# z and h as pairs of blocks, the first chunk's sums a tile later, and h turned between the units of the last chunk, in a hybrid encoder block of split fp32 matmuls

## The chip, the core and the metric

The kernel runs on one core of one Trainium2 chip. TensorE does the matmuls, and it also turns (transposes) blocks by multiplying them with the identity. VectorE and ScalarE make operands for it and empty its PSUM banks, GpSimd takes a few helper jobs, and SyncE issues most of the DMAs. Each engine works through its own instructions in the order in which they stand. The metric is the device time of one execution in microseconds (us), lower is better. Times shown are medians of runs, the profiled execution is one run more.

## The reference, cut to what matters

```python
D_MODEL, SEQ, D_FF = 2048, 512, 4 * 2048

def rms_norm(x, gain):
    return x * lax.rsqrt(jnp.mean(x * x, axis=-1, keepdims=True) + EPS) * gain

def reference(...):
    h = x
    ...                       # gated convolutions: mixed
    o = jnp.einsum("bse,ed->bsd", mixed, w_out)
    h = h + rms_norm(o, mix_post_gain)
    m = rms_norm(h, mlp_pre_gain)
    z = jnp.square(jax.nn.relu(jnp.einsum("bsd,df->bsf", m, w_up)))
    z = jnp.einsum("bsf,fd->bsd", z, w_down)
    return h + rms_norm(z, mlp_post_gain)
```

All is float32. Tokens are 512, so that a block of 128 features by 512 tokens takes 256 KB, 2 KB on each of 128 partitions.

## The kernel before, in words

**Numbers.** Every float32 operand is split into a high part (ScalarE rounds it, L94 for activations, L237 for weights) and a low part (VectorE subtracts, L95 and L242). A product is three matmuls: high by low, low by high, high by high.

**Stages.** Input projection, convolutions, output projection, up projection, down projection. The up projection gives z in 64 blocks of 128 features by 512 tokens. Most of them are made two at a time by Strassen's scheme with seven products (`by_seven`, products in L296). After the last sum ScalarE takes relu and square and stores each block to `z_dram` on its own queue (`relu_squared`). The 16 blocks of h had gone to `h_dram` in the same layout, features on partitions.

**Down projection.** It has features of the output on the free axis: the stationary operand is a block of z (128 features by 128 tokens), the moving one 512 columns of w_down. Its 64 z blocks go in 8 chunks of 8.

- Chunks 0 to 6: two tiles of the output (`wide_tile`, t = 0 and 1: 4 banks for the 4 groups of 128 tokens, 8 blocks, so 8 x 4 x 3 = 96 matmuls in L889 to L891), then the other half of the output by seven products (`wide_seven`, 7 x 24 matmuls). A unit of weights is 128 x 1024, two blocks; each unit of a `wide_tile` is 24 matmuls. After a tile the banks are copied (chunk 0) or added (later) to the running totals.
- The seven products also need sums of neighbouring blocks of z, `t_z`, four pairs in a chunk. `strassen_sums` (L332) makes them on VectorE from a pair of blocks that `load_pair` (L883) loads from DRAM once more, and splits them (L94, L95). `chunk_block` orders this: while tile t = 0 takes its blocks, it loads a pair at one block and makes its sums at the next.
- The blocks of z for a chunk are loaded one by one into `scratch` (256 KB, 8 buffers named tmp) by `load_z` (L824) and split two steps later. `prepare_z` lists these steps for the next chunk, and `z_step(n)` does n of them: three after each of the seven products, for chunk 0 within the last seven products of the up projection.
- The last chunk takes four `wide_tile`s with its first four blocks (8 units of 24 matmuls) and then, after h has been turned, the final part: for each group of 128 tokens b and each tile t, four blocks (12 matmuls), the last sum, and for each b the norm and the writing of the output.
- h is wanted with tokens on partitions. So between the last chunk's tiles and the final part come four transposes of the norm (L1000) and 64 of h: 16 loads of one block (L1017, into tmp), per bank four transposes (L1021), then one ScalarE copy into a slot (L1025).

**What sets the order.** No scheduler moves anything: each engine executes its instructions in the order in which the program writes them, and `evacuate` puts an evacuation off to the next `run_pending`. SyncE issues all loads of weights, z and h on one queue in that order; a load waits there until its buffer is free, and all behind it wait too. Weights go through 6 buffers named raw (L122). `W.take(n, AHEAD)` hands out n units and prepares units up to AHEAD further on. PSUM has 7 banks, and there are 43 slots of 4 KB per partition for split operands, sums and totals. The few rows named `small` and the identity are from pools of their own or from scratch.

Of the kernel before, what the change touches and what calls it, by code (L numbers as in the profile page):

```python
# [13 lines left out]
P = 128  # L14
# [44 lines left out]
def encoder_block(  # L59
# [279 lines left out]
    def evacuate(f, *args):  # L339
        pending.append(lambda: f(*args))  # L340
# [478 lines left out]

    z, z_raw = {}, {}  # L820

    def load_z(k):
        z_raw[k] = scratch()
        nc.sync.dma_start(z_raw[k], z_dram[:, k * S : (k + 1) * S])  # L824

    def split_z(k):
        z[k] = split_pair(z_raw.pop(k))
# [2 lines left out]

    def prepare_z(c):

        for i in range(CHUNK + 2):
            for f, behind in ((load_z, 0), (split_z, 2)):
                if 0 <= i - behind < CHUNK:
                    z_steps.append(lambda f=f, k=c * CHUNK + i - behind: f(k))

    def z_step(n):
        while n > 0 and z_steps:
            z_steps.popleft()()  # L840
            n -= 1
# [9 lines left out]
    for m in range(UP_PLAIN, N_UP, 2):  # L851
        if m == N_UP - 2:
            prepare_z(0)
            evacuate(z_step, 2)
        by_seven(
            up_product,
            *(scratch() for _ in range(2)),
            *((lambda c, m=n: relu_squared(m, c, c)) for n in (m, m + 1)),
            z_step,
        )  # L860
# [15 lines left out]
            for i in range(2):  # L876
                total[t, 2 * n + i] = pair[:, i, :]

    def load_pair(c, i):
        pair = scratch(), scratch()  # L880
        for n, t in enumerate(pair):
            k = c * CHUNK + 2 * i + n
            nc.sync.dma_start(t, z_dram[:, k * S : (k + 1) * S])  # L883
        return pair

    def wide(ps, z_hi, z_lo, part, n, first, last):

        hi, lo = (w[:, n * WIDE : (n + 1) * WIDE] for w in part)
# [3 lines left out]

    tokens = lambda n: slice(n * P, (n + 1) * P)

    def wide_tile(t, first_sum, blocks, make_moving, step):

        pss = [bank() for _ in range(TB)]
        for n in range(0, len(blocks), 2):
            (part,) = W.take(1, AHEAD)
            run_pending()  # L900
            for i in range(2):
                moving = make_moving(blocks[n + i])
                for b, ps in enumerate(pss):
                    wide(
                        ps, *both(moving, tokens(b)), part, i,
                        n + i == 0, n + i == len(blocks) - 1,
                    )
            step()
        for b, ps in enumerate(pss):
            evacuate(accumulate, first_sum, total[t, b], ps)  # L910

    def wide_seven(c):

        if c == 0:
            for _ in range(7):
                seven.append(slot([P, 2, WIDE]))
        for q, name in enumerate(("r10", "t10", "t11", "t20", "t21", "r21", "r20")):
            parts = W.take(2, AHEAD)
            run_pending()
            n, half = int(name[1]) - 1, int(name[2]) * TB // 2  # L920
            right = lambda i: z[c * CHUNK + 2 * i + n] if name[0] == "r" else t_z[i][n]
            for j in range(2):
                ps = bank()
                for i in range(CHUNK // 2):
                    wide(
                        ps, *both(right(i), tokens(half + j)), parts[i // 2], i % 2,
                        i == 0, i == CHUNK // 2 - 1,
                    )
                evacuate(accumulate, c == 0, seven[q][:, j, :], ps)
            z_step(3)  # L930

    def combine():
        p1, p5, p6, p7, p4, p3, p2 = seven
# [8 lines left out]
            total[3, j], total[3, 2 + j] = p4[:, j, :], p7[:, j, :]  # L942
        return deque(steps)

    AHEAD = 4
    run_pending()
    for c in range(N_CHUNK):
        pairs = deque(range(CHUNK // 2))
        waiting = []

        def chunk_block(k):
            while c * CHUNK + k not in z:
                z_step(1)
            if c < N_CHUNK - 1:
                if waiting:
                    i, even, odd = waiting.pop()
                    t_z[i] = strassen_sums(even, odd)
                elif pairs:
                    i = pairs.popleft()
                    waiting.append((i, *load_pair(c, i)))  # L960
            return z[c * CHUNK + k]

        if c == N_CHUNK - 1:
            break
        for t in range(2):
            if c == 0:
                new_total(t)
            wide_tile(t, c == 0, range(CHUNK), chunk_block, lambda: None)
        prepare_z(c + 1)
        wide_seven(c)  # L970


    steps = combine()

    def combine_step():
        for _ in range(4):
            if steps:
                pending.append(steps.popleft())

    for t in range(N_WIDE):  # L980
        wide_tile(t, False, range(CHUNK // 2), chunk_block, combine_step)

    gains = [slot([P, 2, WIDE]) for _ in range(2)]
    for n, t in enumerate(gains):
# [3 lines left out]
            .partition_broadcast(P)  # L988
            .rearrange("p o (a b) -> p (o a) b", a=2),
        )  # L990
    identity = scratch(P)
    nc.gpsimd.memset(identity, 1.0)
    nc.gpsimd.affine_select(
        out=identity, in_=identity, pattern=[[1, P]], compare_op=ALU.is_equal, fill=0.0, base=0,
        channel_multiplier=-1,
    )
    norm_2, norm_4 = (new(small, [P, TB], F32, "four") for _ in range(2))
    ps = bank()
    for b in range(TB):
        nc.tensor.transpose(ps[:, tokens(b)], norm["h 2"][:, tokens(b)], identity)  # L1000
    for b in range(TB):
        nc.scalar.activation(norm_2[:, b : b + 1], ps[:, b * P : b * P + 1], AF.Copy)
    nc.vector.tensor_tensor(norm_4, norm_2, norm_2, op=ALU.mult)
# [6 lines left out]
    h_back = {}  # L1010

    def turn(t):

        h = [scratch() for _ in range(4)]
        for i in range(4):
            k = 4 * t + i
            nc.sync.dma_start(h[i], h_dram[:, k * S : (k + 1) * S])  # L1017
        for b in range(TB):
            ps = bank()
            for i in range(4):  # L1020
                nc.tensor.transpose(ps[:, tokens(i)], h[i][:, tokens(b)], identity)  # L1021
            if b % 2 == 0:
                pair = slot([P, 2, WIDE])
            h_back[t, b] = pair[:, b % 2, :]
            nc.scalar.activation(h_back[t, b], ps, AF.Copy)  # L1025

    for t in range(N_WIDE):
        turn(t)
# [40 lines left out]
    for b in range(TB):  # L1069
        gained = {}  # L1070
        for t in range(N_WIDE):
            run_pending()
            ps = bank()
            for i in range(CHUNK // 2):
                k = CHUNK // 2 + i
                wide(
                    ps, *both(chunk_block(k), tokens(b)), parts[t, i // 2], i % 2,
                    i == 0, i == CHUNK // 2 - 1,
                )
# [84 lines left out]
```

## Time and profile before

| | |
|---|---|
| median of 3 runs | 1990.6 us (1989.06 to 1991.93) |
| the profiled execution, its own time | 1991.09 us |
| its span from first to last instruction | 1989.3 us (1.8 us lie around it) |
| TensorE clock granted, mean | 0.994 of full |
| TensorE (PE) busy | 1947.4 us, 98% |
| VectorE (DVE) busy | 1545.2 us, 78% |
| ScalarE (ACT) busy | 815.8 us, 41% |
| GpSimd (POOL) busy | 97.8 us, 5% |
| moved by DMA | 272.55 MB |
| chain of work that ended last | PE 93%, DVE 3%, DMA 2%, ACT 1% |

How to read it: the span is the profiled execution's first instruction to its last, and the time adds a constant around it. The chain is followed backwards from the last instruction, at each step to what released it. With PE busy for 98% of the span and holding 93% of the chain, what is left to look at are the places where PE waits or runs at a lower clock. The clock is told as a share of full: the two levels are 1.2 GHz (0.50) and 2.4 GHz (1.00). In the windows of a trace "x" counts instructions that touch the window, so that one may count in two windows.

### The profile page before, as it was taken

Reading aid. Unit: us, or ns where it says so; the run is one execution under the profiler, and the core shown is the slowest. Engines: PE = TensorE matmul, PEld = TensorE weight load, DVE = VectorE, ACT = ScalarE, POOL = GpSimd, SP = SyncE. Lnnn points to the kernel's source line nnn. Section 1 sums busy time; section 2 is a strip of 40 time slices with the busy share of each in tenths; the row PEclk is TensorE's granted clock in tenths of the full one; section 3 lists DMA queues with packets and bytes.
Section 4 is the critical chain, followed back from the end, with each engine's and each line's share of the span. In section 5 each row is a group of like instructions: output and inputs, shape, how many; then the busy total and the mean of one; then the engine's idle time right before and its main releaser. Section 6 shows DMA issues by size and latency. Waiting matters only on the chain.

```text
span 1989.3 us, 28150 instructions
## 1 busy us (share of the span) xinstructions
PE 1947.4 (98%) x11224; PEld 1720.6 (86%) x11224; DVE 1545.2 (78%) x2000; ACT 815.8 (41%) x1091; POOL 97.8 (5%) x86
## 2 busy tenths in 40 slices
PE   8999999999999899999999999989999999999988
PEld 6888888888998689999999999978888888888876
DVE  7899989668786887777777777675788687877937
ACT  6222112343444555454544444446344243332422
POOL 4000010200210400000000000000000000000000
PEclk9999999999999999999999999999999999999989
DMA  7232322232446434343433434454354363552532
GB/s 252 89 107 86 105 97 102 88 115 75 138 144 242 165 107 158 108 146 120 138 128 127 139 115 151 165 175 165 122 184 139 125 212 117 170 165 100 186 127 85
DMA packets 95315, 272.55 MB, mean 137 GB/s; under 512 B 10704, under 2 KB 12880, under 8 KB 95184
## 3 DMA queue, kind: packets, MB, share of 16 engines
q1 hardware_dynamic: 81360, 245.93, 37.6%
q10 hardware_dynamic: 13824, 24.82, 3.3%
q8 instruction: 88, 1.44, 0.3%
q14 instruction: 43, 0.35, 0.1%
HBM read 241.87 MB, written 28.84 MB: 136 GB/s over the span
## 4 chain that ended last, share of the span: by engine, by line
PE 93%; DVE 3%; DMA 2%; ACT 1%; issue 1%; SPq 0%; DVEq 0%; ACTq 0%
PE bank L296 56%; PE bank L890 11%; PE bank L891 11%; PE bank L889 11%; PE bank L316 1%; PE bank L315 1%; PE bank L314 1%; DVE slot L694 1%; DMA raw<-w_in_in 1%; DVE slot L242 1%; DVE slot L692 1%; DMA tmp<-h_dram 0%; PE bank L1021 0%; DVE slot L98 0%; PE sums L380 0%
## 5 line engine op out<-in xcount | busy, mean ns | idle before, releaser
L296 PE MATMUL bank<-slot,slot 128*128 128x256 f32 (+1 forms) x7584 | 1128.2, 311 | 0.0
L296 PEld LDWEIGHTS bank<-slot,slot 128*128 128x128 f32 x7584 | 1047.1, 191 | 80.5 <-issue 1.9
L242 DVE TENSOR_TENSOR slot<-raw,slot 128x1024 fp32r<-128x1024 f32 x332 | 414.1, 1263 | 44.7 <-ACT slot L237 38.4
L237 ACT ACTIVATE slot<-raw 128x1024 fp32r<-128x1024 f32 x332 | 338.9, 1048 | 151.1 <-DVE raw L212 67.4
L889 PE MATMUL bank<-slot,slot 128*128 128x512 f32 x968 | 377.7, 390 | 6.2 <-ACT slot L94 6.2
L890 PE MATMUL bank<-slot,slot 128*128 128x512 f32 x968 | 377.6, 390 | 0.5 <-DVE slot L95 0.5
L891 PE MATMUL bank<-slot,slot 128*128 128x512 f32 x968 | 377.2, 390 | 0.0
L237 ACT ACTIVATE slot<-slot 128x1024 fp32r<-128x1024 f32 x170 | 176.8, 1057 | 330.1 <-PE bank L296 161.0
L242 DVE TENSOR_TENSOR slot<-slot,slot 128x1024 fp32r<-128x1024 f32 x170 | 210.8, 1240 | 75.2 <-PE bank L889 59.7
L889 PEld LDWEIGHTS bank<-slot,slot 128*128 128x128 f32 x968 | 182.2, 188 | 44.7 <-ACT slot L94 6.9
L890 PEld LDWEIGHTS bank<-slot,slot 128*128 128x128 f32 x968 | 182.1, 188 | 39.1 <-DVE slot L95 1.3
L891 PEld LDWEIGHTS bank<-slot,slot 128*128 128x128 f32 x968 | 182.1, 188 | 37.8
L94 ACT ACTIVATE slot<-tmp 128x512 fp32r<-128x512 f32 (+1 forms) x160 | 91.3, 611 | 277.2 <-DVE tmp L332 140.0
L332 DVE TENSOR_TENSOR tmp<-tmp,bank 128x256 f32<-128x256 f32 x224 | 93.9, 419 | 112.5 <-PE bank L296 111.4
L498 DVE SCALAR_TENSOR_TENSOR slot<-slot,par_sb,slot 128x512 f32<-128x512 f32 x240 | 162.9, 744 | 0.0
L332 DVE TENSOR_TENSOR slot<-slot,bank 128x512 f32<-128x512 f32 x164 | 107.5, 682 | 59.5 <-PE bank L891 59.5
L95 DVE TENSOR_TENSOR slot<-tmp,slot 128x512 fp32r<-128x512 f32 (+1 forms) x160 | 102.0, 673 | 30.0 <-ACT slot L94 29.7
L316 PE MATMUL bank<-slot,slot 128*128 128x512 f32 (+1 forms) x216 | 82.2, 381 | 10.0 <-DVE slot L98 9.9
L314 PE MATMUL bank<-slot,slot 128*128 128x512 f32 (+1 forms) x216 | 82.1, 380 | 7.5 <-ACT slot L94 6.8
L405 POOL TENSOR_TENSOR sum<-sum,tmp 128x512 f32<-128x512 f32 x50 | 75.9, 1518 | 120.3 <-ACT tmp L409 118.8
L315 PE MATMUL bank<-slot,slot 128*128 128x512 f32 (+1 forms) x216 | 80.9, 375 | 0.3 <-DVE slot L95 0.3
L165 DVE TENSOR_TENSOR slot<-raw,raw 128x1024 f32<-128x1024 f32 x64 | 78.0, 1218 | 0.0
(101 smaller groups left out, 876.1 us busy)
## 6 DMA issues: line engine op xcount, KB each, us to landing
raw<-w_up_in SPq DMA_DIRECT2D x128, 512.0 KB, 5.2
raw<-w_down_in SPq DMA_DIRECT2D x128, 512.0 KB, 4.2
raw<-w_in_in SPq DMA_DIRECT2D x76, 512.0 KB, 4.2
tmp<-z_dram SPq DMA_DIRECT2D x120, 256.0 KB, 4.6
raw<-w_out_in SPq DMA_DIRECT2D x32, 512.0 KB, 4.4
z_dram<-tmp ACTq DMA_DIRECT2D x64, 256.0 KB, 5.4
tmp<-x_in SPq DMA_DIRECT2D x16, 256.0 KB, 4.4
slot<-x_in SPq DMA_DIRECT2D x8, 512.0 KB, 7.7
```

The costliest lines, as they stand in the source:

```text
L95: nc.vector.tensor_tensor(lo, value, hi.bitcast(F32), op=ALU.subtract)
L237: nc.scalar.activation(hi, value, AF.Copy)
L242: nc.vector.tensor_tensor(lo, value, hi.bitcast(F32), op=ALU.subtract)
L296: nc.tensor.matmul(ps, s, m, start=n == 0, stop=n == len(todo) - 1)
L314: nc.tensor.matmul(ps[:, cols], hi, mhi, start=first, stop=False)
L315: nc.tensor.matmul(ps[:, cols], lo, mhi, start=False, stop=False)
L316: nc.tensor.matmul(ps[:, cols], hi, mlo, start=False, stop=last)
L332: add = lambda out, a, b, op=ALU.add: nc.vector.tensor_tensor(out, a, b, op=op)
L498: nc.vector.scalar_tensor_tensor(out=acc, in0=g[:, k : k + S], scalar=w, in1=acc, op0=ALU.mult, op1=ALU.add)
L889: nc.tensor.matmul(ps, z_hi, lo, start=first, stop=False)
L890: nc.tensor.matmul(ps, z_lo, hi, start=False, stop=False)
L891: nc.tensor.matmul(ps, z_hi, hi, start=False, stop=last)
```

## The change

- **Loads as pairs.** `z_pair(k)` loads blocks k and k+1 in one DMA of 512 KB into one slot; `load_z` and the loads for the sums use it. The tmp buffers no longer take z. A chunk's preparation is 4 loads and 8 splits, 12 steps, where it was 8 and 8. It begins at the third of the seven products (`if q > 1`), where it began at the first. In the up projection the two steps ahead of the last seven products go away.
- **Sums.** In chunk 0 tile t = 0 makes none and prepares weights only one unit ahead. The sums' loads and sums come after the units of tile t = 1, one pair per unit, the last after the tile. In the other chunks they start behind the first unit of tile t = 0, and a pair's sums follow a unit after its load, where it was a block after it.
- **h.** The identity and the four transposes of the norm stand ahead of the last chunk. h is loaded as 8 pairs into slots, four of them ahead of the last chunk and the others on the way. After each of the 8 units of the last chunk's tiles, `last_step` turns two banks (8 transposes in L1012, 2 copies in L1013), loads ahead, and puts off the steps of `combine` as before. What was between the tiles and the final part is gone, except the loads of the gains (now behind the tiles) and the last weight units.
- Number and shape of all matmuls and transposes are the same; SyncE issues 68 loads fewer for the same bytes.

```diff
+    def z_pair(k):
+        t = slot([P, 2, S])
+        nc.sync.dma_start(t, z_dram[:, k * S : (k + 2) * S].rearrange("p (a b) -> p a b", a=2))
+        return t[:, 0, :], t[:, 1, :]
+
     def load_z(k):
-        z_raw[k] = scratch()
-        nc.sync.dma_start(z_raw[k], z_dram[:, k * S : (k + 1) * S])
+        z_raw[k], z_raw[k + 1] = z_pair(k)
...
     def prepare_z(c):
-        for i in range(CHUNK + 2):
-            for f, behind in ((load_z, 0), (split_z, 2)):
-                if 0 <= i - behind < CHUNK:
-                    z_steps.append(lambda f=f, k=c * CHUNK + i - behind: f(k))
+        for k in range(c * CHUNK, (c + 1) * CHUNK + 2, 2):
+            if k < (c + 1) * CHUNK:
+                z_steps.append(lambda k=k: load_z(k))
+            if k > c * CHUNK:
+                z_steps.extend((lambda k=n: split_z(k)) for n in (k - 2, k - 1))
...
             prepare_z(0)
-            evacuate(z_step, 2)
...
-            (part,) = W.take(1, AHEAD)
+            (part,) = W.take(1, ahead)
...
-            z_step(3)
+            if q > 1:
+                z_step(3)
...
+    def chunk_block(k):
+        while k not in z:
+            z_step(1)
+        z_step(2)
+        return z[k]
+
+    for c in range(N_CHUNK - 1):
+        sums, waiting = deque(range(CHUNK // 2)), []
+        def z_sums():
+            if waiting:
+                i, pair = waiting.pop()
+                t_z[i] = strassen_sums(*pair)
+            if sums:
+                i = sums.popleft()
+                waiting.append((i, z_pair(c * CHUNK + 2 * i)))
+
         for t in range(2):
             if c == 0:
                 new_total(t)
-            wide_tile(t, c == 0, range(CHUNK), chunk_block, lambda: None)
+            early = c == 0 and t == 0
+            wide_tile(
+                t, c == 0, range(c * CHUNK, (c + 1) * CHUNK), chunk_block,
+                (lambda: None) if early else z_sums, 1 if early else 4,
+            )
+            if sums and not early:
+                z_sums()
+        z_sums()
         prepare_z(c + 1)
         wide_seven(c)
...
+    def turn(t, b):
+        if b % 2 == 0:
+            pair = slot([P, 2, WIDE])
+            h_back[t, b], h_back[t, b + 1] = pair[:, 0, :], pair[:, 1, :]
+        ps = bank()
+        for i in range(4):
+            nc.tensor.transpose(ps[:, tokens(i)], h_raw[t, i][:, tokens(b)], identity)
+        nc.scalar.activation(h_back[t, b], ps, AF.Copy)
+
+    turns = deque((t, b) for t in range(N_WIDE) for b in range(TB))
+
+    def last_step():
+        for _ in range(2):
+            turn(*turns.popleft())
+        if turns and turns[0][1] == 0 and turns[0][0] + 1 < N_WIDE:
+            load_h(turns[0][0] + 1)
         for _ in range(4):
             if steps:
                 pending.append(steps.popleft())
+    load_h(0)
+    load_h(1)
+    turn_norm()
+    at = (N_CHUNK - 1) * CHUNK
     for t in range(N_WIDE):
-        wide_tile(t, False, range(CHUNK // 2), chunk_block, combine_step)
+        wide_tile(t, False, range(at, at + CHUNK // 2), chunk_block, last_step)
```

In the rows that follow, a number behind a name is that of a buffer in the program.

SyncE's queue from the last products of the up projection on, before; slot, tmp and raw are the buffers, L824 loads a block of z, L883 one of a pair for the sums:

```order
L122 DMA raw_12526<-w_down_in 128x1024
L122 DMA raw_12558<-w_down_in 128x1024
L824 DMA tmp_12562<-z_dram 128x512
L122 DMA raw_12593<-w_down_in 128x1024
L824 DMA tmp_12602<-z_dram 128x512
L122 DMA raw_12646<-w_down_in 128x1024
L122 DMA raw_12652<-w_down_in 128x1024
L883 DMA tmp_12654<-z_dram 128x512
L883 DMA tmp_12655<-z_dram 128x512
L122 DMA raw_12698<-w_down_in 128x1024
L824 DMA tmp_12700<-z_dram 128x512
```

The same place now, L825 loads two blocks of z:

```order
L122 DMA raw_12522<-w_down_in 128x1024
L122 DMA raw_12554<-w_down_in 128x1024
L825 DMA slot_12558<-z_dram 128x1024
L122 DMA raw_12589<-w_down_in 128x1024
L825 DMA slot_12595<-z_dram 128x1024
L825 DMA slot_12638<-z_dram 128x1024
L825 DMA slot_12658<-z_dram 128x1024
L122 DMA raw_12712<-w_down_in 128x1024
L122 DMA raw_12742<-w_down_in 128x1024
```

All eight blocks of chunk 0 are now on the queue before the weights that wait for VectorE, and no load for the sums stands there.

VectorE at the end of the up projection and the start of the down projection, before; L332 with four rows from tmp_12654 and tmp_12655 is the first pair's sums, L95 the low parts of z and of the sums, L242 those of weights:

```order
L95 TENSOR_TENSOR slot_12599<-tmp_12393,slot_12599 128x512
L95 TENSOR_TENSOR slot_12604<-tmp_12395,slot_12604 128x512
L332 TENSOR_TENSOR tmp_12379<-tmp_12379,bank_12607 128x256
L242 TENSOR_TENSOR slot_12644<-raw_12462,slot_12589 128x1024
L242 TENSOR_TENSOR slot_12650<-raw_12464,slot_12642 128x1024
L332 TENSOR_TENSOR tmp_12670<-tmp_12654 128x256
L332 TENSOR_TENSOR tmp_12671<-tmp_12655,tmp_12654 128x256
L332 TENSOR_TENSOR tmp_12670<-tmp_12655,tmp_12670 128x256
L332 TENSOR_TENSOR tmp_12671<-tmp_12670,tmp_12655 128x256
L95 TENSOR_TENSOR slot_12676<-tmp_12670,slot_12676 128x512
L95 TENSOR_TENSOR slot_12679<-tmp_12671,slot_12679 128x512
L242 TENSOR_TENSOR slot_12696<-raw_12526,slot_12648 128x1024
```

The same place now:

```order
L95 TENSOR_TENSOR slot_12597<-slot_12558,slot_12597 128x512
L95 TENSOR_TENSOR slot_12600<-slot_12558,slot_12600 128x512
L332 TENSOR_TENSOR tmp_12379<-tmp_12379,bank_12603 128x256
L95 TENSOR_TENSOR slot_12640<-slot_12595,slot_12640 128x512
L95 TENSOR_TENSOR slot_12655<-slot_12595,slot_12655 128x512
L95 TENSOR_TENSOR slot_12672<-slot_12638,slot_12672 128x512
L95 TENSOR_TENSOR slot_12675<-slot_12638,slot_12675 128x512
L95 TENSOR_TENSOR slot_12690<-slot_12658,slot_12690 128x512
L95 TENSOR_TENSOR slot_12693<-slot_12658,slot_12693 128x512
L242 TENSOR_TENSOR slot_12710<-raw_12458,slot_12585 128x1024
```

Before, blocks 2 and 3 of z were split behind the first pair's sums; now all eight blocks are split first, and the sums follow far behind.

TensorE at the end of the last chunk's tiles, before; tmp_17462 to tmp_17465 are blocks of h, tmp_17429 is the identity:

```order
L889 MATMUL bank_17362<-slot_17257,slot_17004 128x512
L890 MATMUL bank_17362<-slot_17217,slot_17004 128x512
L891 MATMUL bank_17362<-slot_17217,slot_17004 128x512
L1000 MATMUL bank_17434<-tmp_17429,rstd_5686 128x128 x4
L1021 MATMUL bank_17470<-tmp_17429,tmp_17462 128x128
L1021 MATMUL bank_17470<-tmp_17429,tmp_17463 128x128
L1021 MATMUL bank_17470<-tmp_17429,tmp_17464 128x128
L1021 MATMUL bank_17470<-tmp_17429,tmp_17465 128x128
```

TensorE after the first unit of the last chunk, now; slot_17028 and slot_17030 are pairs of blocks of h, L887 to L889 are the matmuls of `wide`:

```order
L887 MATMUL bank_17049<-slot_16936,slot_16878 128x512
L888 MATMUL bank_17049<-slot_16892,slot_16878 128x512
L889 MATMUL bank_17049<-slot_16892,slot_16878 128x512
L1012 MATMUL bank_17083<-tmp_17023,slot_17028 128x128 x2
L1012 MATMUL bank_17083<-tmp_17023,slot_17030 128x128 x2
L1012 MATMUL bank_17089<-tmp_17023,slot_17028 128x128 x2
L1012 MATMUL bank_17089<-tmp_17023,slot_17030 128x128 x2
L887 MATMUL bank_17046<-slot_16942,slot_16883 128x512
L888 MATMUL bank_17046<-slot_16934,slot_16883 128x512
```

The 64 transposes of h have gone from one run behind the tiles to eight runs of eight, one behind each unit.

## Rows read from the trace of the kernel before

**Rows 1.** Waits of PE, whole span: us in all, times, longest.

```profile
PE bank L889 <- ACT slot L94: 6.2, 1, 6.2
PE bank L1021 <- DMA tmp<-h_dram: 6.0, 3, 3.0
PE bank L1021 <- ACT slot L1025: 2.5, 1, 2.5
```

**Rows 2.** Windows of the down projection: us, busy PE, PEld, DVE, ACT, POOL (instructions), PEclk, DMA, GB/s.

```profile
1298.24:1304.58 6.34, 0.16 (x2) 0.00 (x1) 3.62 (x7) 2.67 (x5) 0.00 (x0) 0.83 1.00 376
1304.58:1309.48 4.90, 4.62 (x11) 3.29 (x12) 4.57 (x10) 2.64 (x5) 0.00 (x0) 0.53 0.70 224
1309.48:1916.50 607.02, 607.02 (x2679) 502.58 (x2678) 458.33 (x590) 231.90 (x293) 0.62 (x2) 1.00 0.46 152
1916.50:1936.60 20.10, 11.69 (x69) 10.34 (x68) 7.09 (x9) 10.95 (x22) 0.00 (x0) 0.75 0.37 118
```

**Rows 3.** Timeline of PE at the start: start, us, engine, line, operation, [wait].

```profile
1298.01 0.39 PE L891 MATMUL bank<-slot,slot 128*128 128x512 f32 x1
1304.58 0.80 PE L889 MATMUL bank<-slot,slot 128*128 128x512 f32 x1 [6.18 <-ACT slot L94]
1309.48 0.40 PE L890 MATMUL bank<-slot,slot 128*128 128x512 f32 x1
```

**Rows 4.** The chain that ended last, 1290 to 1305: start, us, what.

```profile
1295.36 0.42 SPq L883
1295.88 5.16 DMA tmp<-z_dram
1301.05 0.77 DVE tmp L332 x2
```

**Rows 5.** Timeline of SP's queue at the end of the up projection.

```profile
1256.40 26.16 SPq L122 DMA_DIRECT2D raw<-w_down_in  x6
1282.72 0.33 SPq L824 DMA_DIRECT2D tmp<-z_dram  x1
1285.11 0.33 SPq L122 DMA_DIRECT2D raw<-w_down_in  x1
```

**Rows 6.** Timeline of PE and ACT around the turning of h.

```profile
1917.36 2.97 ACT L237 ACTIVATE slot<-raw 128x1024 fp32r<-128x1024 f32 x3
1935.21 1.64 PE L1021 MATMUL bank<-tmp,tmp 128*128 128x128 f32 x13 [1.46 <-DMA tmp<-h_dram]
1936.60 0.48 PE L889 MATMUL bank<-slot,slot 128*128 128x512 f32 x1
1936.91 0.40 PE L890 MATMUL bank<-slot,slot 128*128 128x512 f32 x1
```

**Rows 7.** Windows within the turning of h, columns as in rows 2.

```profile
1930.07:1933.80 3.73, 3.67 (x16) 3.27 (x16) 0.00 (x0) 2.39 (x4) 0.00 (x0) 0.50 0.50 160
1933.80:1935.20 1.40, 0.00 (x0) 0.00 (x0) 0.00 (x0) 0.00 (x0) 0.00 (x0) 0.98 0.40 145
1935.20:1936.60 1.40, 1.39 (x13) 1.40 (x14) 0.00 (x0) 1.03 (x3) 0.00 (x0) 1.00 0.00 0
```

**Rows 8.** DVE groups by line and form, 1309.5 to 1374: busy us, mean ns | idle before.

```profile
L242 DVE TENSOR_TENSOR slot<-raw,slot 128x1024 fp32r<-128x1024 f32 x12 | 14.5, 1219 | 11.2 <-ACT slot L237 11.2
L95 DVE TENSOR_TENSOR slot<-tmp,slot 128x512 fp32r<-128x512 f32 x16 | 10.4, 688 | 10.1 <-ACT slot L94 10.1
L332 DVE TENSOR_TENSOR tmp<-tmp,tmp 128x256 f32<-128x256 f32 x6 | 2.4, 422 | 0.1
```

**Rows 9.** Groups by line and form, 1830 to 1916: accumulation on DVE.

```profile
L332 DVE TENSOR_TENSOR slot<-slot,bank 128x512 f32<-128x512 f32 x30 | 19.8, 683 | 12.2 <-PE bank L891 12.2
```

**Rows 10.** Line L1025 on ACT: shortest, median, longest ns, first and last start.

```profile
L1025 ACT ACTIVATE slot<-bank x16: 591/598/647, 1920.2 to 1937.0; 128x512 f32<-128x512 f32 x16
```

**Rows 11.** DMA issues, 1250 to 1330: count, KB each, median us to landing.

```profile
raw<-w_down_in SPq DMA_DIRECT2D x14, 512.0 KB, 4.0
tmp<-z_dram SPq DMA_DIRECT2D x19, 256.0 KB, 4.2
```

More of the change, by code (lines that the diff above doesn't have):

```diff
@@ L877, in new_total @@
                 total[t, 2 * n + i] = pair[:, i, :]
[L879 to L884, printed above, removed]
     def wide(ps, z_hi, z_lo, part, n, first, last):
@@ L893, in encoder_block, with wide_tile @@
     tokens = lambda n: slice(n * P, (n + 1) * P)
-    def wide_tile(t, first_sum, blocks, make_moving, step):
+    def wide_tile(t, first_sum, blocks, make_moving, step=lambda: None, ahead=4):
         pss = [bank() for _ in range(TB)]
         for n in range(0, len(blocks), 2):
-            (part,) = W.take(1, AHEAD)
+            (part,) = W.take(1, ahead)
             run_pending()
@@ L917, in wide_seven @@
         for q, name in enumerate(("r10", "t10", "t11", "t20", "t21", "r21", "r20")):
-            parts = W.take(2, AHEAD)
+            parts = W.take(2, 4)
             run_pending()
@@ L943, in combine @@
         return deque(steps)
-    AHEAD = 4
     run_pending()
[L947 to L964, printed above, removed]
+    def chunk_block(k):
[12 more added lines that the diff above has]
+                waiting.append((i, z_pair(c * CHUNK + 2 * i)))
         for t in range(2):
@@ L973, in encoder_block, with load_h, turn_norm @@
     steps = combine()
-    def combine_step():
+    identity = scratch(P)
+    nc.gpsimd.memset(identity, 1.0)
+    nc.gpsimd.affine_select(
+        out=identity, in_=identity, pattern=[[1, P]], compare_op=ALU.is_equal, fill=0.0, base=0,
+        channel_multiplier=-1,
+    )
+    norm_2, norm_4 = (new(small, [P, TB], F32, "four") for _ in range(2))
+    h_raw, h_back = {}, {}
+    def load_h(t):
+        for n in range(2):
+            pair, k = slot([P, 2, S]), 4 * t + 2 * n
+            nc.sync.dma_start(
+                pair, h_dram[:, k * S : (k + 2) * S].rearrange("p (a b) -> p a b", a=2)
+            )
+            h_raw[t, 2 * n], h_raw[t, 2 * n + 1] = pair[:, 0, :], pair[:, 1, :]
+    def turn_norm():
+        ps = bank()
+        for b in range(TB):
+            nc.tensor.transpose(ps[:, tokens(b)], norm["h 2"][:, tokens(b)], identity)
+        for b in range(TB):
+            nc.scalar.activation(norm_2[:, b : b + 1], ps[:, b * P : b * P + 1], AF.Copy)
+        add(norm_4, norm_2, norm_2, ALU.mult)
+    def turn(t, b):
+        if b % 2 == 0:
+            pair = slot([P, 2, WIDE])
+            h_back[t, b], h_back[t, b + 1] = pair[:, 0, :], pair[:, 1, :]
+        ps = bank()
+        for i in range(4):
[7 more added lines that the diff above has]
+            load_h(turns[0][0] + 1)
         for _ in range(4):
@@ L990, in encoder_block @@
         )
[L991 to L1003, printed above, removed]
     parts = {}
@@ L1009, in encoder_block @@
     run_pending()
[L1010 to L1028, printed above, removed]
     nc.scalar.activation(warm, eps, AF.Abs_reciprocal_sqrt)
@@ L1076, in encoder_block @@
                 wide(
-                    ps, *both(chunk_block(k), tokens(b)), parts[t, i // 2], i % 2,
+                    ps, *both(chunk_block(at + k), tokens(b)), parts[t, i // 2], i % 2,
                     i == 0, i == CHUNK // 2 - 1,
```

## The prediction, made before the changed kernel ran

> **What bounds the kernel now.** I read the table of engines first: PE is busy for 98% of the span and holds 93% of the chain that ended last, so only what makes PE wait or clocks it down can be won. The waits of PE come next [rows 1]: one wait of 6.2 us stands on L889, the first products of the down projection, 8.5 us stand on L1021, the turning of h. Windows around these two places [rows 2] show a gap at either end of the down projection and between them 607.02 us in which PE is busy without a break at clock 1.00, 0.2266 us per matmul (607.02 / 2679).
>
> **The head gap.** The 24th matmul starts at 1298.01, the 25th at 1304.58 after 6.18 us of waiting for ScalarE's split of block 2, the 35th at 1309.48 [rows 3]; the clock in that stretch was 0.53 [rows 2]. Without a break the 35th would have started 11 x 0.2266 = 2.49 us after the 24th, at 1300.50. The gap costs **8.98 us**. The chain [rows 4] tells why: SyncE issued the loads for the first pair of sums at 1295.36, they landed 5.16 us later, and VectorE, which takes its work in order, stood at the sums with the splits of blocks 2 and 3 queued behind them.
>
> **The tail gap.** From the first transpose of the norm (1916.50) to the first matmul of the final part (1936.60) lie **20.10 us**, in which PE does 68 transposes [rows 2]. Three waits for h (6.0 us), one for a bank (2.5) [rows 1] and the low clock fill it: 16 transposes took 3.67 us at clock 0.50 (0.229 each), and 13 took 1.39 us at 1.00 (0.107 each) [rows 7].
>
> **The change at the head.** What it removes there is the sums in tile t = 0: the two loads and, per pair, four L332 of 0.422 and two L95 of 0.688 [rows 8], 3.06 us of VectorE ahead of blocks 2 and 3. In their place stand six splits of z, which need only their pair. Is it there in time? SyncE gave out block 2 at 1282.72, behind six weight loads, and the next weight load at 1285.11 [rows 5]; a pair takes the first place and the other three stand right behind that weight load. The 512 KB of a unit landed in 4.0 us, 256 KB of z in 4.2 [rows 11], so a pair costs no more delay than a block: the last of them, issued after 1285.4, would land by about 1291, and even twice the 4 us for three pairs at once gives 1294. PE wants block 2 at 1298.24 (24th start plus 0.2266), after a split of 0.688 on VectorE. I take the whole gap: **-8.98 us**. Bounds: nothing (the pairs wait for slots) and all.
>
> Chunk 0's sums move to tile t = 1. By then VectorE has, between the start of that tile and the first product that uses a sum, four sums of 3.06 = 12.2 us and some six units of weight work at 1.219 [rows 8] = 7.3, together 19.6. PE does 96 matmuls of tile 1 and the 24 of the first product (which takes z) in 120 x 0.2266 = 27.2. Slack 7.6 us: I take 0. If the last sums were late by their whole length, up to 12.2 us would come back. Preparing weights one unit ahead instead of four in tile 0 only lets VectorE take z first. ScalarE has the weights' high parts ready well within 24 matmuls (5.44 us) per unit.
>
> **The middle.** PE never waits from 1309.48 to 1916.50, so the new order of loads and sums there can only lose. Per chunk the engines have the same work, sums come a unit (24 matmuls) after their loads instead of half a unit, and the 52 z loads fewer on SyncE's queue were nobody's wait. VectorE is busy 458.33 of 607.02 us and the DMA 0.46 [rows 2]. The one thing new is that z now takes slots, which weights use too. I take 0; a loss is a rival below.
>
> **The change at the tail.** The 20.10 us go. What comes instead is 4 + 64 transposes within the tiles, at full clock 68 x 0.107 = 7.28 us [rows 7], and nine returns from transposes to wide matmuls: at 1936.60 one such return took 0.31 us to the next matmul's start [rows 6], 0.08 more than 0.2266, so 0.75 for nine. Cost 8.03, gain **-12.07**. At the price of a wide matmul per transpose it would be 68 x 0.2266 = 15.4, gain 4.7; without the returns 12.8.
>
> What must lie under cover for that: the ScalarE copies of a unit, 2 x 0.598 [rows 10] and one L237 of 0.99 (2.97 for three [rows 6]), 2.2 of the 6.4 us that PE spends per unit. Inside a tile the four banks of the tile and two of the turn make six of seven. Between tiles four new banks are wanted while the last four are still emptied by accumulations (0.683 each [rows 9]) and the turn's two by copies; the first tile after a turn needs a turn's bank at its third or fourth bank, some 0.7 us behind, a little more than one copy. That is the tightest place; four such tile ends, bound 1 us each.
>
> In the old gap ScalarE also made the last three weight units' high parts (2.97 us [rows 6]), VectorE the low ones and the last four accumulations. These now stand beside the final part. A tile of it takes 12 matmuls and two of the eight units, so the sixth unit is wanted after 30 matmuls (6.8 us), and the first bank that those accumulations empty after 36 (8.2). Three low parts of 1.219 [rows 8] and four accumulations of 0.683 [rows 9] are 6.4 us of VectorE in all, under both. VectorE thus starts 6.4 us late on sums of 2 x 0.683 = 1.37 per tile, which takes PE 2.72; it gains 1.35 per tile and has caught up after five of 16, so the end behind the last matmul is as before. I take 0, bound 3 us. The DMAs of h, 8 x 512 KB, lie where the DMA has room (0.46 busy).
>
> **The sum.** Span 1989.3 - 8.98 - 12.07 = 1968.2; with the 1.8 us around it the profiled execution would go from 1991.1 to 1970.0. It lies 0.5 above the median of the runs, so the median comes to 1969.5 to 1970. I say **1970**.
>
> **A rule against it.** The rows: PE did nothing but transposes from 1916.50 on; the clock was 0.50 to 1933.80, 0.98 in the idle stretch behind that and 1.00 in the next, in which 13 transposes took 0.107 each [rows 7]. So here the full clock came back behind transposes, and they ran at it. The Trainium skill, "TensorE: Matmul & The Clock Gate", section "Part 4: PE-mode transpose", says that a transpose isn't counted as PE activity as a matmul is, that the full clock doesn't engage for it, and that one takes about 275 ns in a kernel. By that figure 68 would cost 18.7 us, an estimate from the page, and the time be 1981. The trace differs in both price and clock, and I go by the trace; the mechanism stays as a rival below, since eight transposes between two groups of 24 matmuls are nowhere in the trace.
>
> **The rivals.**
> - *Turns stall PE*: a copy of a turn sits behind an L237 on ScalarE or a bank comes free late; 1 us at each of eight turns gives 1978. For it: PE waited 2.5 us for just such a copy [rows 1]. Against it: that was with all banks in turns.
> - *The pairs are late*, so that the change doesn't do at the head what it says: 512 KB wait for slots that PE's last products of the up projection still read. The gap stays: 1979. For it: PE reads most slots to the end of that stage. Against it: splits and weights took slots from the same pool there in time.
> - *Sums late*: the second product of chunk 0 waits for VectorE, up to 12.2 us: 1982. Against it: the slack of 7.6.
> - *Slower: slots run short.* With z pairs waiting in slots, weights are prepared a unit later in each of the seven chunks, and PE stands for a unit of 24 matmuls: 7 x 5.44 = 38 us, 2008. It decides from 21.1 / 7 = 3.0 us per chunk on. For it: 43 slots must now hold up to four pairs of unsplit z as well. Against it: PE waits for nothing in the 607 us, and a pair is read by two splits and then free.
> - *Slower: the clock falls* behind each turn, and the last chunk's 192 matmuls go at half speed: 192 x 0.2266 = 43.5 us on top, 2013. It decides from 21.1 us, half of that stretch. Against it: rows 7.
>
> **How the numbers follow.** Forecast (both gaps close) 0.75, turns stall 0.08, sums late 0.05, pairs late 0.05, slots short 0.04, clock falls 0.03. About 0.2% (4 us) is what a measurement here can tell from no change. Faster has the first four, 0.93; the slow two have most of their price above no change, 0.05; 0.02 lies between. The range: below, transposes without returns and a median as low as the lowest run's (1.5 less), 1967; above, transposes at the price of matmuls give 1977.3, and the stalls 1978, so 1979 holds the forecast, the stalls and the late pairs, 0.88 together, of which some lies beyond the points named.
>
> **What would show it.** Right: no wait of PE at 1298 and none from there to the end; the 35th matmul of the stage some 9 us earlier; eight runs of eight transposes in the last chunk, 0.9 to 1.0 us each, at clock 1.00; the same 9 us behind the last matmul. Wrong: a wait of L887 for an L95 of block 2 or 4 (head), a wait in chunk 0's second product for L332 (sums), waits of L1012 or of the next tile's first banks for L1013 (turns), waits spread over all chunks for L242 (slots), a clock below 1.00 in the last chunk (clock).

## The result, and the profile after

| | before | changed |
|---|---|---|
| median | 1990.93 us (1989.06 to 1991.93) | 1969.74 us (1969.51 to 1971.04) |
| ratio to before | | 0.9896, 95% interval 0.9879 to 0.9913 |
| span of the profiled execution | 1989.3 us | 1968.2 us |
| mean granted clock | 0.994 | 0.996 |

The time fell by 21.2 us, 1.0%; the span by 21.1. (The median of the kernel before is of four runs here, of three in the table further up.) The prediction had said 1970.0 and a span of 1968.2.

The waits of PE after (us in all, times, longest). The wait of 6.2 us at the third block and all waits at the turning of h [rows 1] are gone; what is left belongs to earlier stages, apart from 0.2 us.

```profile
PE bank L316 <- DVE slot L98: 9.6, 10, 3.0
PE bank L314 <- ACT slot L94: 8.0, 2, 6.1
PE bank L315 <- DVE slot L95: 0.3, 1, 0.3
PE bank L888 <- DVE slot L95: 0.2, 1, 0.2
```

PE at the start of the down projection after. The 24th matmul starts at 1297.83, the 25th 0.23 us later, the 35th at 1300.32.

```profile
1291.94 0.50 PE L887 MATMUL bank<-slot,slot 128*128 128x512 f32 x1
...
1297.83 0.39 PE L889 MATMUL bank<-slot,slot 128*128 128x512 f32 x1
1298.06 0.39 PE L887 MATMUL bank<-slot,slot 128*128 128x512 f32 x1
...
1300.32 0.39 PE L888 MATMUL bank<-slot,slot 128*128 128x512 f32 x1
```

PE at the first turns in the last chunk after: eight transposes, then the next unit's matmuls; and the last turns, behind which the final part begins.

```profile
1869.72 1.03 PE L1012 MATMUL bank<-tmp,slot 128*128 128x128 f32 x8
1870.51 0.47 PE L887 MATMUL bank<-slot,slot 128*128 128x512 f32 x1
1870.83 0.39 PE L888 MATMUL bank<-slot,slot 128*128 128x512 f32 x1
...
1914.19 1.03 PE L1012 MATMUL bank<-tmp,slot 128*128 128x128 f32 x8
1914.98 0.48 PE L887 MATMUL bank<-slot,slot 128*128 128x512 f32 x1
```

Windows after (us, busy PE, PEld, DVE, ACT, POOL, PEclk, DMA, GB/s): from the 35th matmul to the norm's transposes, the last chunk with all turns, and the final part. PE is busy throughout, at clock 1.00, where [rows 2] showed 0.53 and 0.75 at the two gaps.

```profile
1300.32:1863.82 563.50, 563.50 (x2488) 466.55 (x2487) 434.62 (x565) 226.78 (x288) 0.62 (x2) 1.00 0.46 158
1863.82:1914.98 51.16, 51.16 (x262) 43.02 (x260) 28.50 (x38) 15.62 (x27) 0.00 (x0) 1.00 0.47 165
1914.98:1958.80 43.82, 43.78 (x195) 35.93 (x193) 36.66 (x70) 15.46 (x38) 0.00 (x0) 1.00 0.20 73
```

The two profiled executions, stretch by stretch:

| stretch | before, us | after, us | difference |
|---|---|---|---|
| up to the first matmul of the down projection | 1292.18 | 1291.94 | -0.24 |
| first to 35th matmul | 17.30 | 8.38 | -8.92 |
| 35th matmul to the final part | 607.02 + 20.10 | 614.66 | -12.46 |
| first to last matmul of the final part | 43.39 | 43.39 | 0 |
| last matmul to the end | 9.31 | 9.83 | +0.52 |
| sum | | | -21.10 |

### The profile page after: what moved, and what is told of

It is laid out like the page before. It is cut to its first block, busy times and chain, and to the rows that moved or that the text cites. A ratio compares the mean times of both kernels' runs of the same rounds, so it can differ in the third digit from the quotient of the medians.

```text
span 1968.2 us, 28036 instructions
## 1 busy us (share of the span) xinstructions
PE 1940.5 (99%) x11224; PEld 1717.5 (87%) x11224; DVE 1542.1 (78%) x2000; ACT 815.5 (41%) x1091; POOL 99.8 (5%) x86
## 4 chain that ended last, share of the span: by engine, by line
PE 95%; DVE 3%; DMA 1%; issue 0%; ACT 0%; SPq 0%; ACTq 0%; DVEq 0%
PE bank L296 57%; PE bank L888 11%; PE bank L889 11%; PE bank L887 11%; PE bank L316 2%; PE bank L315 2%; PE bank L314 1%; DVE slot L694 1%; DVE slot L692 1%; DMA raw<-w_in_in 0%; DVE slot L242 0%; PE bank L1012 0%; PE sums L380 0%; DVE slot L98 0%; DMA tmp<-x_in 0%
## 5 line engine op out<-in xcount | busy, mean ns | idle before, releaser
L242 DVE TENSOR_TENSOR slot<-raw,slot 128x1024 fp32r<-128x1024 f32 x332 | 412.7, 1260 | 57.0 <-ACT slot L237 50.7
L887 PE MATMUL bank<-slot,slot 128*128 128x512 f32 x968 | 377.6, 390 | 0.1
L889 PE MATMUL bank<-slot,slot 128*128 128x512 f32 x968 | 376.8, 389 | 0.0
L242 DVE TENSOR_TENSOR slot<-slot,slot 128x1024 fp32r<-128x1024 f32 x170 | 210.8, 1240 | 56.7 <-PE bank L887 38.5
L889 PEld LDWEIGHTS bank<-slot,slot 128*128 128x128 f32 x968 | 181.7, 188 | 37.8
L887 PEld LDWEIGHTS bank<-slot,slot 128*128 128x128 f32 x968 | 181.7, 188 | 37.7 <-ACT slot L94 0.3
L332 DVE TENSOR_TENSOR tmp<-tmp,bank 128x256 f32<-128x256 f32 x224 | 93.8, 419 | 112.5 <-PE bank L296 111.4
L94 ACT ACTIVATE slot<-tmp 128x512 fp32r<-128x512 f32 x96 | 54.1, 607 | 274.6 <-DVE tmp L332 144.3
L332 DVE TENSOR_TENSOR slot<-slot,bank 128x512 f32<-128x512 f32 x164 | 106.0, 681 | 22.2 <-PE bank L889 22.1
L95 DVE TENSOR_TENSOR slot<-slot,slot 128x512 fp32r<-128x512 f32 (+1 forms) x80 | 49.6, 659 | 45.6 <-ACT slot L94 45.6
```

The costliest lines, as they stand in the source:

```text
L242: nc.vector.tensor_tensor(lo, value, hi.bitcast(F32), op=ALU.subtract)
L332: add = lambda out, a, b, op=ALU.add: nc.vector.tensor_tensor(out, a, b, op=op)
L887: nc.tensor.matmul(ps, z_hi, lo, start=first, stop=False)
L889: nc.tensor.matmul(ps, z_hi, hi, start=False, stop=last)
```

## The experiments

Each was timed beside the kernel before on its chip, which came to 1990.6 to 1991.8 us; times are medians.

**Each part alone.** First, h stays behind the last chunk as before, and only the work on z is changed:

```diff
     for t in range(N_WIDE):
-        wide_tile(t, False, range(at, at + CHUNK // 2), chunk_block, last_step)
+        wide_tile(t, False, range(at, at + CHUNK // 2), chunk_block, combine_step)
...
+    for t in range(N_WIDE):
+        turn(t)
```

> Pairs and the deferred sums as in the change, h turned behind the last chunk as before. Theory (two gaps, each closed by its own part): no wait of PE at the third block of the down projection, 20.1 us from the last chunk's tiles to the final part as before, so 1990.9 - 8.9 = 1982 us. Rival (the gains hang together, since the gap at the end only moves work that the other part freed, or pairs in slots disturb the chunks): anything above 1985, or a gap at the end that is not 20 us.

Measured: 1981.57 us, ratio 0.9948 (0.9931 to 0.9964). The 35th matmul started 8.36 us after the first, as in the changed kernel, and the waits at the turning of h were all there:

```profile
PE bank L1028 <- DMA tmp<-h_dram: 5.0, 4, 1.9
PE bank L1028 <- ACT slot L1032: 2.5, 1, 2.5
```

Second, only the work on h is changed, and z is loaded, split and summed as before:

```diff
-        wide_tile(t, False, range(CHUNK // 2), chunk_block, combine_step)
+        wide_tile(t, False, range(CHUNK // 2), chunk_block, last_step)
...
-    for t in range(N_WIDE):
-        turn(t)
```

> z loads and sums as before, h loaded as pairs and turned between the units of the last chunk. Theory: the gap of 8.9 us at the start stays, the 20.1 us at the end give way to about 7.6 us of transposes within the tiles, so 1990.9 - 12.4 = 1978.5 us. Rival (turning between units is only free because of the other part's fewer loads): waits of PE for the turns' banks or for h, time above 1981.

Measured: 1978.5 us, ratio 0.9934 (0.9919 to 0.9949). The gap at the start stayed, and no wait stood at the turns; the row of its waits is that of [rows 1]:

```profile
PE bank L889 <- ACT slot L94: 6.2, 1, 6.2
```

The gains are 10.3 and 13.3 against the same runs of before, 23.6 together where both at once gave 21.2. Each has an interval of some 3 us to either side, so that is additive as far as it can be told; each gap closes by its own part.

**What closes the gap at the start.** The part on z has three edits: pairs, sums a tile later, weights one unit ahead. The last was not run alone. Pairs alone, with the sums still ahead of the splits of blocks 2 and 3:

```diff
+    def load_z(k):
+        z_raw[k], z_raw[k + 1] = z_pair(k)
...
     def load_pair(c, i):
-        pair = scratch(), scratch()
-        for n, t in enumerate(pair):
-            k = c * CHUNK + 2 * i + n
-            nc.sync.dma_start(t, z_dram[:, k * S : (k + 1) * S])
-        return pair
+        return z_pair(c * CHUNK + 2 * i)
```

> Loads of z as pairs in slots, but the sums of chunk 0 in their old place, ahead of the splits of blocks 2 and 3, and h turned as before. Theory (the order of the work on VectorE makes the gap, not the size of the loads): PE still waits for the split of block 2, 5 to 9 us of gap, time 1986 to 1992. Rival (the single loads were the cause): gap under 2 us, time about 1982.

Measured: 1991.15 us, ratio 0.9996 (0.9986 to 1.0005): nothing gained. The wait is the same:

```profile
PE bank L890 <- ACT slot L94: 6.3, 1, 6.3
```

The changed kernel with chunk 0's sums in its first tile, a unit after their load, and weights four units ahead:

```diff
-            early = c == 0 and t == 0
+            early = False
```

> The changed kernel, but chunk 0 makes its sums from the first tile on, a unit after the pair's load, as the other chunks do, and prepares weights four units ahead there too. The splits of blocks 2 and 3 stand ahead of the sums on VectorE all the same. Theory (what counts is that the splits stand ahead of the sums): gap under 1 us, time 1970 to 1971. Rival (the sums must leave the first tile altogether): a wait of PE of 3 us or more within the first 96 matmuls, time 1973 to 1979.

Measured: 1970.9 us, ratio 0.9895 (0.9881 to 0.991); the 35th matmul came 8.83 us after the first, 0.45 later than in the changed kernel. The sums need not leave the first tile. They did stand behind the splits there, and not only behind those of blocks 2 and 3: on VectorE those of blocks 4 to 7 came before the first sum as well.

```profile
1300.92 2.58 DVE L95 TENSOR_TENSOR slot<-slot,slot 128x512 fp32r<-128x512 f32 x4 [1.12 <-ACT slot L94]
1303.81 0.76 DVE L332 TENSOR_TENSOR tmp<-slot 128x256 f32<-128x256 f32 x2 [0.31 <-DMA slot<-z_dram]
```

The kernel before, with no edit but that chunk 0 makes its sums in its second tile:

```diff
-            if c < N_CHUNK - 1:
+            if c < N_CHUNK - 1 and not (c == 0 and tile == 0):
                 if waiting:
...
         for t in range(2):
+            tile = t
```

> The kernel before, with one edit: chunk 0 makes no sums in its first tile, and makes all four in its second. Loads of z stay single blocks, weights stay four units ahead, h is turned as before. Theory (VectorE's order makes the gap): the wait of 6.2 us at block 2 shrinks to 2 or less, since only the weights' parts prepared ahead still stand before the split; the whole gap goes from 8.9 to some 2 us and the time from 1991 to about 1984. Rival (the single loads stand behind weights on the queue, so the wait only moves to block 4): gap of 5 us or more, time 1987 to 1991.

Measured: 1982.4 us, ratio 0.9953 (0.9939 to 0.9968). Single blocks came in time; the 25th matmul waited 0.59 us, and the 35th came 9.79 after the first:

```profile
1296.94 0.39 PE L891 MATMUL bank<-slot,slot 128*128 128x512 f32 x1
1297.92 0.50 PE L889 MATMUL bank<-slot,slot 128*128 128x512 f32 x1 [0.59 <-ACT slot L94]
...
1300.85 0.40 PE L890 MATMUL bank<-slot,slot 128*128 128x512 f32 x1
```

The 1.4 us that are left here (9.79 against 8.38) go with the order too: before it split block 2, ScalarE still made the high parts of three weight units, where it made two in the run above (0.45 left) and none in the changed kernel.

```profile
1294.39 2.96 ACT L237 ACTIVATE slot<-raw 128x1024 fp32r<-128x1024 f32 x3 [0.40 <-ACT tmp L768]
1297.26 1.13 ACT L94 ACTIVATE slot<-tmp 128x512 fp32r<-128x512 f32 x2
```

So the order on VectorE and ScalarE made the gap, and no run shows the size of the loads to have a part in it. That the sums wait for a load of their own, and the splits of loaded blocks behind them, is all but 1.4 us of it.

**What closes the gap at the end.** The changed kernel, with h loaded early but all turns in one run behind the tiles:

```diff
+    unit = []
+
     def last_step():
-        for _ in range(2):
-            turn(*turns.popleft())
-        if turns and turns[0][1] == 0 and turns[0][0] + 1 < N_WIDE:
-            load_h(turns[0][0] + 1)
+        unit.append(0)
+        if len(unit) in (2, 4):
+            load_h(1 + len(unit) // 2)
...
     run_pending()
+    while turns:
+        turn(*turns.popleft())
```

> The changed kernel with its early loads of h as pairs, but all 64 transposes of h in one run behind the last chunk's tiles, as before. It tells how much of the 20.1 us was waiting for h and how much is the run itself. Theory (ScalarE's 16 copies of 0.598 and three weight parts of 0.99, 12.5 us, bind a run of transposes through the banks): 10 to 13 us between tiles and final part, time 1972 to 1976. Rival one (waiting for h was all): 7.6 us as in the changed kernel, 1970. Rival two (the run falls to the low clock for its whole length): 15 us or more, 1977 and above.

Measured: 1969.89 us, ratio 0.9891 (0.9876 to 0.9905), the changed kernel's time. My theory fell, rival one held. PE did all 64 transposes at a stretch, 1907.25 to 1914.15, at clock 1.00. ScalarE's 16 copies ended 1.7 us later and never held PE up:

```profile
1907.25:1914.15 6.90, 6.90 (x65) 6.90 (x64) 0.89 (x2) 6.21 (x13) 0.00 (x0) 1.00 0.00 0
1907.94 7.95 ACT L1013 ACTIVATE slot<-bank 128x512 f32<-128x512 f32 x16 [7.60 <-PE bank L1012]
```

I had priced a copy at 0.598 and put three weight parts in front. Back to back, 16 copies took 7.95, 0.497 each, and the weight parts had been made before, the last at 1899.29. In the kernel before they could not be: there the copies of the norm's transposes (L1002) stand ahead of them on ScalarE, and these had to wait until PE had finished the tiles. The weight parts [rows 6] then held up the first copies of h, which is the wait of 2.5 us for a bank in [rows 1]. This wait stays, at 2.5 us, in each of the three runs that turn the norm and h in the old place, and is gone in all that turn the norm ahead of the last chunk; no run separates that from the loads of h. The first row is from the kernel before, the second from this run:

```profile
1917.14 0.36 ACT L1002 ACTIVATE four<-bank 128x1 f32<-128x1 f32 x4 [33.56 <-PE bank L1000]
1899.29 1.06 ACT L237 ACTIVATE slot<-raw 128x1024 fp32r<-128x1024 f32 x1 [2.11 <-PE bank L889]
```

The changed kernel with h as 16 single blocks in tmp, a unit ahead of their turns:

```diff
     def load_h(t):
-        for n in range(2):
-            pair, k = slot([P, 2, S]), 4 * t + 2 * n
...
+        for i in range(4):
+            h_raw[t, i], k = scratch(), 4 * t + i
+            nc.sync.dma_start(h_raw[t, i], h_dram[:, k * S : (k + 1) * S])
...
-        if turns and turns[0][1] == 0 and turns[0][0] + 1 < N_WIDE:
-            load_h(turns[0][0] + 1)
+        if turns and turns[0][1] == 0:
+            load_h(turns[0][0])
...
     load_h(0)
-    load_h(1)
```

> The changed kernel with h loaded as 16 single blocks into tmp, four at a time and one unit ahead of their turns, instead of as pairs in slots further ahead. Theory (a unit of 5.4 us covers a load of 4 to 5 us): no wait at the turns or under 1 us each, time 1970 to 1973. Rival (the early pairs are what closes the gap at the end): waits of the transposes for h of 2 us or more at each of three tiles, time 1976 or more.

Measured: 1969.67 us, ratio 0.9889 (0.9874 to 0.9904), no wait of PE at the turns. So neither the place of the turns nor the pairs in slots is needed: either the loads go well ahead, or matmuls stand between a load and its turn. What the kernel before lacked was both: loads of h waited 24.4 us on SyncE's queue for buffers that only the turns before them gave free, and no matmuls stood between these loads and the next turns. Such a wait on the queue does no harm by itself: in this run it was 29.2 us, but PE had a unit of matmuls to do before each turn. The first row is from the kernel before, the second from this run:

```profile
SPq L1017 <- PE bank L1021: 24.4, 6, 16.7
SPq L992 <- PE bank L1009: 29.2, 3, 10.2
```

**The price of a transpose, and the clock.** Every transpose of h done four times, 192 more:

```diff
-        for i in range(4):
+        for i in list(range(4)) * 4:
             nc.tensor.transpose(ps[:, tokens(i)], h_raw[t, i][:, tokens(b)], identity)
```

> The changed kernel with every transpose of h done four times into the same bank, 192 more. It prices one and shows the clock under runs of 32 transposes. Theory (0.0985 us each and clock 1.00 throughout): 192 x 0.0985 = 18.9 us more, 1988.6, granted clock 1.00 in the last chunk. Rival (transposes don't hold the clock): the clock falls behind the runs, the following matmuls start 0.43 us apart instead of 0.227, time 2005 or more.

Measured: 1990.66 us, 20.9 more than the changed kernel, 0.109 per transpose. A run of 32 took 3.41 us to the next matmul (0.107 each), and the whole last chunk stood at clock 1.00 with PE busy throughout:

```profile
1869.22 3.65 PE L1012 MATMUL bank<-tmp,slot 128*128 128x128 f32 x32
1872.63 0.48 PE L887 MATMUL bank<-slot,slot 128*128 128x512 f32 x1
...
1863.28:1936.00 72.72, 72.72 (x456) 64.50 (x455) 28.50 (x38) 17.23 (x28) 0.00 (x0) 1.00 0.34 126
```

**A version that beats both.** The transposes cost PE the same wherever they stand, so I took them off PE. VectorE, which has room, transposes each block of h in squares of 32 by 32, and DMAs put the squares in place:

```diff
+    def h_step():
+        if h_turned:
+            m, u = h_turned.pop(0)
+            for a in range(4):
+                f = m * P + 32 * a
+                nc.sync.dma_start(
+                    h_rows[:, f : f + 32].rearrange("(g i) j -> i g j", i=32),
+                    u[32 * a : 32 * a + 32, :].rearrange("p (g j) -> p g j", j=32),
+                )
+        if h_in:
+            m, v = h_in.pop(0)
+            u = scratch()
+            nc.vector.transpose(u, v)
+            h_turned.append((m, u))
+        if h_blocks:
+            m, v = h_blocks.popleft(), scratch()
+            nc.sync.dma_start(v, h_dram[:, m * S : (m + 1) * S])
+            h_in.append((m, v))
...
     def last_step():
-        for _ in range(2):
-            turn(*turns.popleft())
+        load_h(*turns.popleft())
```

> The changed kernel, but TensorE turns no block of h. During chunks 1 to 6 each block of h is loaded, VectorE transposes it in squares of 32 by 32, and four DMAs put the squares in place in DRAM in pieces of 128 bytes; in the last chunk eight loads bring h back with tokens on partitions. Theory (64 transposes cost PE about 0.9 us per eight, 7.2 us in all, wherever they stand, while VectorE and the DMAs have room): 1969.8 - 7.2 = 1962.6. Rival (the small pieces make the DMAs late, so that weights come late in chunks 1 to 6): waits of PE for weights, time 1970 or more.

Beside it the changed kernel once more:

> The changed kernel itself, timed beside the other on the same chip: 1969.7, as on record.

Measured: 1962.38 us, ratio to before 0.986 (0.9845 to 0.9874), against 1969.79, ratio 0.99 (0.9883 to 0.9916), for the changed kernel: 7.4 us less. The rows are from VectorE's groups in chunks 1 to 5, from the DMA issues from 1376 to 1500, and from a window over most of the down projection:

```profile
L967 DVE STREAM_TRANSPOSE tmp<-tmp 128x512 f32<-128x512 f32 x16 | 11.3, 707 | 0.0
...
h_rows<-tmp SPq DMA_DIRECT2D x56, 64.0 KB, 4.0
tmp<-h_dram SPq DMA_DIRECT2D x14, 256.0 KB, 3.9
...
1300.00:1910.00 610.00, 610.00 (x2695) 505.25 (x2694) 478.74 (x627) 239.24 (x305) 0.57 (x2) 1.00 0.54 174
```

VectorE took on 16 x 0.707 = 11.3 us and the DMAs went from 0.46 to 0.54 busy; PE waited for neither. The Trainium skill, "VectorE: DVE Perf Modes", section "The three transpose paths", says that VectorE turns only squares of 32 by 32 within a block and calls that useful for some layouts. That agrees with what had to be added here: 64 DMAs in pieces of 128 bytes, which took about as long for 64 KB (4.0 us, the median of the 56 in that window) as the load of a whole block for 256 KB (3.9).

## Why the prediction was right, point by point

- **The head gap** was put at 8.98 us and all of it taken as gain; 8.92 went. The cause named, sums ahead of the splits on VectorE, is what the runs with pairs alone (nothing gained) and with deferral alone (all but 1.4 of it, which stands behind weight parts) show. The pairs stood where I had put them on SyncE's queue, three behind one weight load:

```profile
1282.41 0.39 SPq L825 DMA_DIRECT2D slot<-z_dram  x1
1284.87 0.33 SPq L122 DMA_DIRECT2D raw<-w_down_in  x1
1285.30 1.59 SPq L825 DMA_DIRECT2D slot<-z_dram  x3
```

 But I had let the pairs share the credit; these runs show none for them.
- **Chunk 0's sums** I took as covered with 7.6 us to spare. The last of them ended at 1331.56 (1330.27 + 1.29), and the first product that uses one began with the 217th matmul, at 1341.58: 10 us to spare.

```profile
1330.27 1.29 DVE L95 TENSOR_TENSOR slot<-tmp,slot 128x512 fp32r<-128x512 f32 x2 [0.24 <-ACT slot L94]
...
1341.58 0.39 PE L887 MATMUL bank<-slot,slot 128*128 128x512 f32 x1
```

- **The middle** was taken as 0 and is 0: no wait in 563.50 us. The rival of short slots has no row.
- **The tail.** 8.03 us of transposes and returns were forecast, 614.66 - 607.02 = 7.64 measured. The term for the transposes was a little large: eight to the next matmul took 0.79, 0.099 each where I had 0.107; the return, 0.09, was right. Gain 12.46 for 12.07. No copy and no bank was late, so the rival of stalls has no row either. The mechanism I gave was incomplete: I listed the waits that filled the 20.10 us and let the new place of the turns remove them. The runs show that early loads of h, with the norm turned ahead of the last chunk, do the same in the old place; the sum came out right because both have the same price. The list of what filled the gap does add up: the four waits are 2.46 + 3.00 + 1.50 + 1.46 = 8.42, and 32 transposes at the low clock cost 32 x (0.229 - 0.108) = 3.9 more than at the full one, together 12.3 of the 12.46 won.
- **The clock rival** (0.03) and the rule of the Trainium skill, "TensorE: Matmul & The Clock Gate", section "Part 4: PE-mode transpose", are decided by rows: PE held clock 1.00 through 64 transposes in a row and paid 0.107 to 0.109 each, where the page has 275 ns and a full clock that doesn't engage. As a duration the page's figure, given for bf16, is near what the trace shows for one transpose, 272 ns; but transposes in a row start 0.1 us apart, and only that spacing is the cost. The trace lists them as matmuls, and whether they use the transpose mode of which the page speaks no run here tells. For the float32 blocks of 128 by 128 of this kernel the measurement decides.

```profile
L1012 PE MATMUL bank<-tmp,slot x64: 270/272/273, 1869.7 to 1914.9; 128*128 128x128 f32 x64
```

 One reading of the prediction needs setting right: it has the clock of the old gap at 0.50 up to 1933.80, as if from the start at 1916.50. The first 16 transposes, in a row, ran at 1.00; the clock was 0.50 only from 1924.90 on, behind waits of 2.46 and 3.00 us with seven transposes between them. So even before the change it was behind waits that the clock fell, not behind transposes. From the kernel before:

```profile
1916.50:1918.40 1.90, 1.90 (x17) 1.67 (x15) 0.87 (x2) 1.26 (x6) 0.00 (x0) 1.00 0.00 0
1918.40:1924.90 6.50, 1.05 (x9) 0.73 (x8) 6.22 (x8) 3.88 (x7) 0.00 (x0) 0.90 0.34 98
1924.90:1928.60 3.70, 3.67 (x16) 3.27 (x16) 0.00 (x0) 2.39 (x4) 0.00 (x0) 0.50 0.40 134
```

- **The final part** was to start 6.4 us late on VectorE and to have caught up after five of 16 sums. Its first sum began 7.77 us after the part's first matmul (1922.75), where before it was 3.02 (1939.62), so 4.8 us late. The fifth sum is the first that waits for PE:

```profile
1926.72 0.68 DVE L332 TENSOR_TENSOR slot<-slot,bank 128x512 f32<-128x512 f32 x1
...
1928.87 0.69 DVE L332 TENSOR_TENSOR slot<-slot,bank 128x512 f32<-128x512 f32 x1 [0.68 <-PE bank L889]
```

- **The end** was said to stay; it grew by 0.52 us, the one term of the sum that was missed. VectorE's and ScalarE's instructions there keep their distance to the last matmul (the first of the last four writes, L1059 before and L1075 after, begins 3.40 and 3.41 us behind it). What differs is the last stores: they landed in 2.5 us at the median, 2.1 before (DMA rows of the last 9 us), and one packet of an instruction queue lies among them:

```profile
q14 instruction: 1, 0.01, 0.2%
h_out<-slot SPq DMA_DIRECT2D x4, 256.0 KB, 2.5
```

 All five profiles with such a packet in the last 9 us end 9.78 to 9.98 us behind the last matmul; the seven without end 9.23 to 9.31 behind it. That this packet delays the stores fits all twelve, but no run took it away by itself, so it stays a reading.

## What to carry to other kernels

When an engine that takes its work in order stalls a faster one, look for an instruction that waits for a late load and has ready work behind it: moving the ready work ahead was worth 7.5 to 8.9 us here, and changing the loads alone nothing. When a stretch of small steps is slow, ask first whether each waits for a buffer that the step before gives free; loading ahead closed the gap in the old place just as interleaving did. What then remains is the steps' own price on the bound engine, and that goes only when another engine takes them.

## What the runs showed of the hardware that was not expected

- A run of 64 transposes of 128 x 128 float32 holds TensorE at clock 1.00, at 0.108 us each.
- ScalarE's copies of a bank (128 x 512) take 0.598 us alone [rows 10] and follow each other every 0.497 us in a run of 16.
- VectorE transposes 128 x 512 float32 in squares of 32 in 0.707 us, about what a subtraction of that size takes (0.688 [rows 8]).
- A DMA of 64 KB in pieces of 128 bytes lands in 4.0 us, about as one of 256 KB in long rows (3.9 in the same window).
